# A decoder step on one core: the conditioning of tiles 5 to 7 in one visit of eight weight blocks, of tiles 8 to 15 in two of eight

## The chip, the cores and the metric

The kernel runs on one core of one Trainium2 chip. The metric is the device time of one execution in microseconds (us), from the first to the last thing that the core does; it is given as the median of several runs.

## The reference, cut to what matters

One layer of a decoder runs over 288 tokens: 256 of a prompt and 8 groups of 4 samples. Each group of tokens (9 in all) has a conditioning vector `c`, from which one matrix product makes six vectors of 2048 numbers per group; they scale, shift and gate the features (2048 = 16 tiles of 128).

```python
mod = (jax.nn.silu(c) @ w_ada + b_ada).reshape(n, N_MOD, 1, D_MODEL)   # w_ada: 2048 x 12288
sh_m, sc_m, gt_m, sh_f, sc_f, gt_f = [mod[:, i] for i in range(N_MOD)]
h = _rms(x, g_mix) * (1 + sc_m) + sh_m
proj = h @ w_in                                                        # 2048 x 9216
```

Behind it come a short convolution, a spatial gate, three products that merge them (`w_pa`, `w_pb`, `w_out`) and a feed-forward block (`w_ffn_in`, `w_ffn_out`). All is float32. The change concerns the first two lines and the product with `w_in`.

## The kernel before, in words

**Main blocks.** A weight matrix is cut into parts of 128x128. A block (class `Blk`) is 12 to 16 such parts, fetched by one DMA of SP into one of 7 raw buffers (tag "raw", `RAW = 7`, 1024 KB each). `Blk.split` then makes of each 4 parts a high half (ACT, line 480) and a low half (DVE; line 258 while these engines run in the order in which the program is written, else 487), into 4 "hi" and 4 "lo" buffers of 4 parts each (`SPB = 4`). The raw buffer is free when the last low half is made. PE takes one part with three matmuls (`triple`, lines 239, 242 and 244): high by high, high by low, low by high, 288 columns each.

**Conditioning blocks.** Class `Ada` does the product with `w_ada`. The unit aD makes the scales and shifts of tiles 5 to 7, in 8 blocks of 768 KB (two of the 16 input tiles each); aE makes those of tiles 8 to 15, in 16 blocks of 1024 KB (one input tile each). PE reads these straight from the raw buffer (line 412): a block is 8 matmuls of 192 columns each in aD and 4 of 512 in aE, counted twice that in the profile's rows, which list weight loads and matmuls; the buffer is free when PE has read it. A run of such blocks between main blocks is called a visit. When a unit's last block is done, `tail` (later, on DVE) adds the bias, and `mk_h1` makes the modulated input tiles `h1`, which the following main blocks read.

**Order.** The product with `w_in` goes over input tiles in the order in which they become ready: `w0`, `wK`, `wA` (tiles 0 to 1, then 2 to 3), `wB` (six blocks of 12 parts, tiles 2 to 4), `wX` (six of 12, tiles 5 to 7), `wS` (five of 14, tiles 1 to 7), `wC` (19 of 12, tiles 2 to 7), then `wE`, `wF`, `wD`. The function `at` puts visits behind the n-th main block of a list. Before the change they are: 4 blocks of aD behind wB1, 4 behind wB3; 5 blocks of aE behind wX3, 6 behind wS4, 5 behind wC6. All of it lies in the first 215 us.

**Loads.** `stream` is the order in which PE uses blocks, `order` that in which SP fetches them. When step i of the stream is written, load i + 7 of `order` is issued, so that each load waits for one of the 7 buffers. In the loop at line 1201 some main blocks are put in front of the visit that they follow, so that they can be fetched and split ahead of it: wA3, wA4, wA5 and wC0.

**Splits.** Up to the step `free` (behind the last visit of aE) the splits are placed by hand: `feed` writes the next split into ACT's and DVE's order when the parts that are split and unused have come down to the block's `lead`, 12 unless set (wC1 has 7); the low half is written two parts later (`LAG`). Evictions of PE's results and the jobs of `pre_h1` and `mk_h1` (line 318 scales one tile) stand in the same two queues.

Of the kernel before, what the change touches and what calls it, by code (L numbers as in the profile page):

```python
# [88 lines left out]
def decoder_kernel(tc, d):  # L89
    nc = tc.nc  # L90
    from contextlib import ExitStack

    with ExitStack() as es:
        def pool(name, bufs=1, **kw):
            return es.enter_context(tc.tile_pool(name=name, bufs=bufs, **kw))

        pc = pool("const")
        pw = pool("wstream")
        pslot = pool("slots", MAIN)
        pkept = pool("kept", KEPT)  # L100
        ptmp = pool("tmp", 5)
        pps = pool("psum", 4, space=bass.MemoryType.PSUM)
        with tc.manual_schedule(engines={nc.tensor.engine}):
            _body(tc, nc, d, pc, pw, pslot, pkept, ptmp, pps)


def _body(tc, nc, d, pc, pw, pslot, pkept, ptmp, pps):
# [208 lines left out]
    def normed(kt, rb):  # L316
        t = slot()
        V.tensor_tensor(t, x[:, kt, :], rb, ALU.mult)
        return t

    def modulate(ks, get, gm, sh0, out):
        hs, his = {}, {}

        def affine(k, t):
            h = tmp()
            hi = slot(F32R)
            A.activation(
                h[:, :TP], t[:, :TP], AF.Identity, bias=mod[:, sh0 + k, 0:1], scale=gm[:, k, 0:1]
            )
            V.tensor_tensor(sam(h[:, TP:]), sam(t[:, TP:]), bc4(gm[:, k, 1:]), ALU.mult)  # L330
            V.tensor_tensor(sam(h[:, TP:]), sam(h[:, TP:]), bc4(mod[:, sh0 + k, 1:]), ALU.add)
            A.copy(hi, h)
            hs[k], his[k] = h, hi

        def finish_(k):
            lo = slot(F32R)
            V.tensor_tensor(lo, hs[k], his[k].bitcast(F32), ALU.subtract)
            out[k] = (his[k], lo)

        ts = {}  # L340
        n = len(ks)
        for i in range(n + 2):
            if i < n:
                ts[i] = get(ks[i])
            if 1 <= i <= n:
                affine(ks[i - 1], ts.pop(i - 1))
            if i >= 2:
                finish_(ks[i - 2])
# [241 lines left out]
    def ada(name):  # L590
        u = units[name]
        return [Ada(u, b) for b in range(16 // u[2])]
# [8 lines left out]
    def warm(n, out=None):  # L601
        out = idle if out is None else out
        for _ in range(n):
            PE.matmul(out[:, :T], wb[:, :P], wb, start=True, stop=True)
# [46 lines left out]
    def pre_h1(k0, k1):  # L651
        def scaled(k):
            def f():
                made[k] = normed(k, S["rb1"])

            return f

        return Do(lambda: jobs.extend(scaled(k) for k in range(k0, k1)), None)

    def make_h1(k0, k1):  # L660

        def scaled(k):
            made[k] = normed(k, S["rb1"])

        def affine(k):
            t, h = made[k], tmp()
            A.activation(h[:, :TP], t[:, :TP], AF.Identity, bias=mod[:, k, 0:1], scale=gm1[:, k, 0:1])
            V.tensor_tensor(sam(h[:, TP:]), sam(t[:, TP:]), bc4(gm1[:, k, 1:]), ALU.mult)
            V.tensor_tensor(sam(h[:, TP:]), sam(h[:, TP:]), bc4(mod[:, k, 1:]), ALU.add)
            made[k] = h  # L670

        def high(k):
            hi = slot(F32R)
            A.copy(hi, made[k])
            made[k] = (made[k], hi)

        def low(k):
            h, hi = made.pop(k)
            lo = slot(F32R)
            V.tensor_tensor(lo, h, hi.bitcast(F32), ALU.subtract)  # L680
            h1[k] = (hi, lo)

        def job(i):
            def f():
                for at, part in enumerate(parts):
                    if k0 <= i - at < k1:
                        part(i - at)

            return f

        parts = (affine, high, low) if k0 in made or jobs else (scaled, affine, high, low)
        jobs.extend(job(i) for i in range(k0, k1 + len(parts) - 1))
# [47 lines left out]
    def gm_of(k0, k1):  # L740
        V.scalar_tensor_tensor(
            gm1[:, k0:k1, :],
            mod[:, 16 + k0 : 16 + k1, :],
            1.0,
            gmix[:, k0:k1].unsqueeze(2).to_broadcast([P, k1 - k0, NC]),
            ALU.add,
            ALU.mult,
        )

    def mk_h1(k0, k1):  # L750
        def f():
            gm_of(k0, k1)
            if S.get("paced") is not None:
                return make_h1(k0, k1)
            modulate(range(k0, k1), lambda k: normed(k, S["rb1"]), gm1, 0, h1)

        return Do(f)
# [3 lines left out]
    def sinkA(m, ps):  # L761
        wide = m < ROOTLESS and m not in LONG
        t = kept() if m in LONG else slot(shape=(P, TU) if wide else (P, T))
        part[m] = t[:, :T]
        w = TU if wide else T
        copy = A.copy if (m not in ON_VECTOR if m < ROOTLESS else m % 2 or m % 8 == 4) else V.tensor_copy
        copy(t[:, :w], ps[:, :w])
        if m < ROOTLESS:
            i = 0 if wide else LONG.index(m)
            e = t[:, T:] if wide else (extra + [extra2])[i // 4][:, i % 4]  # L770
            raws[m] = t, e
            if not wide:
                copy(e, ps[:, T:TU])

    def sinkC(m, ps):
        if m not in raws:
            return sinkB(m, ps)
        t, e = raws.pop(m)
        V.scalar_tensor_tensor(t[:, :TP], ps[:, :TP], e[:, :1], t[:, :TP], ALU.add, ALU.add)  # L779
        rescale(m + 4, V.tensor_tensor(t[:, TP:T], ps[:, TP:T], t[:, TP:T], ALU.add))  # L780
# [7 lines left out]
    def sinkX(m, ps):  # L788
        after = sinkB(m, ps)
        if m >= 68:  # L790
            rescale(m - 68, after)

    def sinkB(m, ps):
        return V.tensor_tensor(part[m], ps[:, :T], part[m], ALU.add)  # L794
# [307 lines left out]
    def at(main, plan):  # L1102
        out, n = [], 0
        for s in main:
            out.append(s)
            if isinstance(s, Blk):
                n += 1
                out += plan.pop(n, [])
        assert not plan
        return out  # L1110

    a0, a1, aC, aD, aE = ada("a0"), ada("a1"), ada("aC"), ada("aD"), ada("aE")
# [6 lines left out]
    wA = [Blk("wA", i, (xe if i < many else h1).__getitem__, lambda m, ps: sinkA(FIRST + m, ps)) for i in range((72 - FIRST) // 8)]  # L1119
    wB = [Blk("wB", i, rh1, lambda m, ps: sinkB(LATER + m, ps)) for i in range((72 - LATER) // 4)]  # L1120
    wX = [Blk("wX", i, rh1, lambda m, ps: sinkX(LATER + m, ps)) for i in range((72 - LATER) // 4)]
    wS = [Blk("wS", i, rh1, sinkC) for i in range(SINGLE // 2)]
    wC = [Blk("wC", i, rh1, lambda m, ps: sinkC(SINGLE + m, ps)) for i in range((LATER - SINGLE) // 2)]
    for b in wA[:many]:
        b.width = TU
    wC[1].lead = 7
    w0.cut = 512
    wK.cut = 384
    w0.lead, wK.lead, wA[0].lead, wA[1].lead = 6, 3, 6, 8
# [2 lines left out]
    steps = [Do(lambda: warm(19)), a0[0], Do(lambda: warm(5)), a0[1]]  # L1132
# [5 lines left out]

    plan = {4: [Do(root, None)], 5: aC[:2], 6: aC[2:5] + [pre_h1(2, 5)], 7: aC[5:] + [mk_h1(2, 5)]}
    steps += at([w0, wK] + wA, plan)  # L1140
    steps += at(wB, {2: aD[:4], 3: [pre_h1(5, 8)], 4: aD[4:] + [mk_h1(5, 8)]})
    free = Do(lambda: None, None)
    steps += at(wX + wS + wC, {4: aE[:5], 11: aE[5:11], 18: aE[11:] + [free, mk_h1(8, 12), mk_h1(12, 16)]})

    def wD(m0, m1):
        return [Blk("wD", i, rh1, sinkD) for i in range(m0 // 2, m1 // 2)]
# [51 lines left out]
    stream = [s for s in steps if not isinstance(s, Do) and not s.apart]  # L1198
    pos = {id(s): i for i, s in enumerate(stream)}
    order = list(stream)  # L1200
    for unit, blk in ((aC[:2], wA[3]), (aC[2:5], wA[4]), (aC[5:], wA[5]), (aE[5:11], wC[0])):
        order.remove(blk)
        order.insert(order.index(unit[0]), blk)
    head = contextlib.ExitStack()
# [163 lines left out]
```

## Time and profile before

| | |
|---|---|
| median of 3 runs | 1591.73 us (1591.66 to 1592.06) |
| the profiled execution | 1592.19 us, of which its span 1590.4 us |
| PE busy | 1579.8 us, 99% of the span |
| PE weight loads, DVE, ACT busy | 96%, 64%, 46% |
| DMA | 357.89 MB, 225 GB/s over the span |

The span is the time from the first to the last instruction of the profiled execution; the rest of its 1592.19 us lies around it. PE's matmuls are pipelined, and a busy PE may still issue late: a delay shows as a longer step from one matmul's start to the next. The chain is the list of work that set the end, followed back from the last instruction. Times in the rows are microseconds from the span's start.

### The profile page before, as it was taken

How to read it: one execution, taken by the hardware profiler on the slowest of the kernel's cores; microseconds unless marked ns; L12 is line 12 of the kernel's file. 1: busy time of each engine (PE TensorE's matmuls, PEld its weight loads, DVE VectorE, ACT ScalarE, POOL GpSimd, SP SyncE). 2: the span in 40 equal slices, each digit the busy share in tenths (PEclk: the TensorE clock that was granted, in tenths of full speed). 3: DMA queues.
4: the chain of work that ended last, by engine and by line, in shares of the span. 5: the costliest groups of instructions: out<-in, count | busy, mean ns of one | idle time of the engine just before them, and what ended most of it. 6: DMA issues, size and time to landing. Idle time of an engine off the chain costs nothing.

```text
span 1590.4 us, 31810 instructions
## 1 busy us (share of the span) xinstructions
PE 1579.8 (99%) x12700; PEld 1519.9 (96%) x12700; DVE 1014.4 (64%) x2200; ACT 736.2 (46%) x1366; POOL 21.4 (1%) x65
## 2 busy tenths in 40 slices
PE   9999999999999999999999999999999999999997
PEld 8999899998999989899898999999999999999997
DVE  6777788877755758567844555555555555555565
ACT  6633344643444435356643444444444444444464
POOL 0000000000000000011000000000000000000000
PEclk9999999999999999999999999999999999999999
DMA  9887876777767778784757356453564534645341
GB/s 382 333 331 281 306 261 217 276 290 296 291 231 266 309 290 264 273 295 164 295 182 275 128 181 212 161 176 113 171 230 159 176 120 164 231 159 175 113 165 60
DMA packets 67685, 357.89 MB, mean 225 GB/s; under 512 B 7632, under 2 KB 19536, under 8 KB 37840
## 3 DMA queue, kind: packets, MB, share of 16 engines
q1 hardware_dynamic: 67248, 355.73, 61.6%
q8 instruction: 99, 1.62, 0.4%
q14 instruction: 50, 0.41, 0.1%
q10 hardware_dynamic: 288, 0.13, 0.0%
HBM read 352.74 MB, written 3.09 MB: 224 GB/s over the span
## 4 chain that ended last, share of the span: by engine, by line
PE 98%; DMA 1%; DVE 0%; DVEq 0%; ACT 0%; issue 0%; ACTq 0%
PE pm L239 31%; PE pm L244 31%; PE pm L242 30%; PE ada L412 5%; DMA raw<-in_wK 1%; DMA raw<-in_w 0%; DVE st L1079 0%; DMA t<-in_c 0%; PE px L242 0%; PE px L239 0%; PE px L244 0%; PE px L911 0%; PE px L910 0%; PE px L857 0%; PE px L213 0%; PE px L1051 0%
## 5 line engine op out<-in xcount | busy, mean ns | idle before, releaser
L239 PE MATMUL pm<-s,hi 128*128 128x288 f32 (+1 forms) x3750 | 1094.8, 292 | 0.0
L242 PE MATMUL pm<-s,hi 128*128 128x288 f32 (+1 forms) x3750 | 1090.5, 291 | 0.0
L244 PE MATMUL pm<-s,lo 128*128 128x288 f32 (+1 forms) x3738 | 1088.1, 291 | 0.0
L480 ACT CAST hi<-raw 128x512 fp32r<-128x512 f32 (+1 forms) x963 | 585.5, 610 | 777.9 <-PE pm L242 743.5
L487 DVE TENSOR_TENSOR lo<-raw,hi 128x512 fp32r<-128x512 f32 (+1 forms) x849 | 577.5, 682 | 408.6 <-ACT hi L480 396.1
L239 PEld LDWEIGHTS pm<-s,hi 128*128 128x128 f32 x3750 | 702.1, 187 | 11.7 <-issue 9.9
L242 PEld LDWEIGHTS pm<-s,hi 128*128 128x128 f32 x3750 | 702.2, 187 | 0.0
L244 PEld LDWEIGHTS pm<-s,lo 128*128 128x128 f32 x3738 | 699.9, 187 | 0.0
L258 DVE TENSOR_TENSOR lo<-raw,hi 128x512 fp32r<-128x512 f32 x111 | 74.4, 676 | 19.8 <-ACT hi L480 18.7
L412 PE MATMUL ada<-raw,cs 128*32 128x512 f32 (+2 forms) x1088 | 80.7, 444 | 1.0 <-DMA raw<-in_a 0.6
L412 PEld LDWEIGHTS ada<-raw,cs 128*32 128x32 f32 x1088 | 29.1, 110 | 41.9 <-issue 37.5
L802 DVE TENSOR_TENSOR s<-pm,s 128x288 f32<-128x288 f32 x72 | 32.8, 456 | 16.3 <-PE pm L244 16.1
L311 ACT CAST s<-t 128x288 fp32r<-128x288 f32 (+1 forms) x76 | 32.9, 433 | 15.6 <-DVE t L834 9.4
L313 DVE TENSOR_TENSOR s<-t,s 128x288 fp32r<-128x288 f32 (+1 forms) x76 | 35.0, 460 | 6.0 <-ACT s L311 5.2
L353 DVE SCALAR_TENSOR_TENSOR x<-pm,mod,x 128x256 f32<-128x256 f32 x79 | 37.6, 475 | 0.0
L1000 DVE SCALAR_TENSOR_TENSOR t<-t,pm 128x288 f32<-128x288 f32 x42 | 19.1, 455 | 19.6 <-PE pm L244 19.6
L794 DVE TENSOR_TENSOR s<-pm,s 128x288 f32<-128x288 f32 x48 | 21.8, 454 | 10.8 <-PE pm L244 10.0
L352 DVE TENSOR_TENSOR t<-pm,mod 128x32 f32<-128x32 f32 x79 | 15.1, 192 | 20.1 <-PE pm L244 19.5
L779 DVE SCALAR_TENSOR_TENSOR s<-pm,s 128x256 f32<-128x256 f32 x36 | 17.3, 481 | 8.3 <-PE pm L244 8.3
L785 DVE TENSOR_TENSOR s<-s,rb 128x288 f32<-128x288 f32 x48 | 21.6, 449 | 0.0
L181 ACT ACTIVATE t<-x 128x288 f32<-128x288 f32 x29 | 12.9, 444 | 17.6 <-DVE x L356 17.6
L186 DVE TENSOR_TENSOR acc<-acc,t 128x288 f32<-128x288 f32 x33 | 15.0, 455 | 8.2 <-ACT t L181 8.2
(170 smaller groups left out, 489.0 us busy)
## 6 DMA issues: line engine op xcount, KB each, us to landing
raw<-in_fi SPq DMA_DIRECT2D x84, 1024.0 KB, 4.8
raw<-in_a SPq DMA_DIRECT2D x56, 1024.0 KB, 5.0
raw<-in_f SPq DMA_DIRECT2D x64, 704.0 KB, 4.0
raw<-in_wD SPq DMA_DIRECT2D x34, 1024.0 KB, 6.7
raw<-in_aE SPq DMA_DIRECT2D x16, 1024.0 KB, 7.0
raw<-in_wo SPq DMA_DIRECT2D x16, 1024.0 KB, 6.0
raw<-in_wC SPq DMA_DIRECT2D x19, 768.0 KB, 6.5
raw<-in_pa SPq DMA_DIRECT2D x8, 1024.0 KB, 9.7
```

The lines of the kernel that those rows point to most:

```text
L239: PE.matmul(out, wh, ah, start=first, stop=False)
L242: end_ = PE.matmul(out, wh, al, start=False, stop=turn and last)
L244: end_ = PE.matmul(out, wl, ah, start=False, stop=last)
L258: lows.pop(0)[1]()
L311: A.copy(hi, a)
L313: V.tensor_tensor(lo, a, hi.bitcast(F32), ALU.subtract)
L353: V.scalar_tensor_tensor(x[:, m, :TP], ps[:, :TP], mod[:, gt0 + m, 0:1], x[:, m, :TP], ALU.mult, ALU.add)
L412: PE.matmul(acc[32 * j : 32 * j + 32, h * w // n : (h + 1) * w // n], cs[:, kt, :], self.held[2 * j + h] if self.held else self.raw[:, o : ...
L480: A.copy(hi, self.raw[:, s * 128 : e * 128])
L487: sub()
L794: return V.tensor_tensor(part[m], ps[:, :T], part[m], ALU.add)
L802: V.tensor_tensor(a, ps[:, :T], a, ALU.add)
```

## The change

The two visits of aD become one of eight blocks behind wB3; the three of aE become two of eight, behind wS4 and wC6. wB4 is now fetched ahead of the visit of aD and wC7 ahead of the second of aE; wC0 stays ahead of the first. wB5 and wC8, like wC1 before, are split when 7 unused parts are left instead of 12. The steps that make h1 stand where they stood.

```diff
@@ -1123,7 +1123,7 @@
-    wC[1].lead = 7
+    wB[5].lead = wC[1].lead = wC[8].lead = 7
@@ -1138,9 +1138,9 @@
-    steps += at(wB, {2: aD[:4], 3: [pre_h1(5, 8)], 4: aD[4:] + [mk_h1(5, 8)]})
+    steps += at(wB, {3: [pre_h1(5, 8)], 4: aD + [mk_h1(5, 8)]})
     free = Do(lambda: None, None)
-    steps += at(wX + wS + wC, {4: aE[:5], 11: aE[5:11], 18: aE[11:] + [free, mk_h1(8, 12), mk_h1(12, 16)]})
+    steps += at(wX + wS + wC, {11: aE[:8], 18: aE[8:] + [free, mk_h1(8, 12), mk_h1(12, 16)]})
@@ -1198,7 +1198,7 @@
-    for unit, blk in ((aC[:2], wA[3]), (aC[2:5], wA[4]), (aC[5:], wA[5]), (aE[5:11], wC[0])):
+    for unit, blk in ((aC[:2], wA[3]), (aC[2:5], wA[4]), (aC[5:], wA[5]), (aD, wB[4]), (aE[:8], wC[0]), (aE[8:], wC[7])):
```

## Rows read from the trace of the kernel before

**Rows 1.** The page, part 1: span, and busy time of each engine.
```profile
span 1590.4 us, 31810 instructions
...
PE 1579.8 (99%) x12700; PEld 1519.9 (96%) x12700; DVE 1014.4 (64%) x2200; ACT 736.2 (46%) x1366; POOL 21.4 (1%) x65
```
**Rows 2.** The page, part 4: the chain that ended last, by engine.
```profile
PE 98%; DMA 1%; DVE 0%; DVEq 0%; ACT 0%; issue 0%; ACTq 0%
```
**Rows 3.** The chain in order of time: start, us, what; visits and a matmul behind one.
```profile
43.37 1.44 PE ada L412 x32
...
84.46 2.74 PE ada L412 x64
87.20 0.33 PE pm L239
...
127.67 4.43 PE ada L412 x40
...
168.85 5.29 PE ada L412 x48
```
**Rows 4.** Stretches: us, PE, PEld, DVE, ACT, POOL busy (instructions), clock, DMA share, GB/s.
```profile
100.00:125.00 25.00, 25.00 (x195) 25.00 (x194) 22.49 (x54) 12.20 (x22) 0.00 (x0) 1.00 0.85 329
```
**Rows 5.** All waits of PE's matmuls for a load, in the whole span: us, times, longest.
```profile
PE ada L412 <- DMA raw<-in_a: 0.6, 1, 0.6
```
**Rows 6.** Timeline of PE: start and length of three visits.
```profile
84.39 2.81 PE L412 MATMUL ada<-raw,cs 128*32 128x192 f32 x64
...
168.78 5.36 PE L412 MATMUL ada<-raw,cs 128*32 128x512 f32 x48
...
206.93 4.50 PE L412 MATMUL ada<-raw,cs 128*32 128x512 f32 x40
```
**Rows 7.** Waits of SP's queue around visits (84.9 to 85.6; 166 to 169.6).
```profile
SPq L385 <- PE ada L412: 0.5, 1, 0.5
...
SPq L463 <- DVE lo L258: 3.6, 1, 3.6
```
**Rows 8.** Timeline of DVE near visits: low halves, and a scaling job.
```profile
83.70 0.68 DVE L258 TENSOR_TENSOR lo<-raw,hi 128x512 fp32r<-128x512 f32 x1
...
97.23 0.45 DVE L318 TENSOR_TENSOR s<-x,rb 128x288 f32<-128x288 f32 x1
...
168.63 0.69 DVE L258 TENSOR_TENSOR lo<-raw,hi 128x512 fp32r<-128x512 f32 x1 [0.69 <-ACT hi L480]
...
206.14 0.68 DVE L258 TENSOR_TENSOR lo<-raw,hi 128x512 fp32r<-128x512 f32 x1
```
**Rows 9.** Timeline of SP: the loads issued as these buffers came free.
```profile
169.35 0.33 SPq L463 DMA_DIRECT2D raw<-in_wC  x1
...
206.85 0.33 SPq L463 DMA_DIRECT2D raw<-in_wC  x1
```
**Rows 10.** DMA issues, us to landing; issued at 169.35, 169.91, 165.33, 836.86, 837.72, 287.34, 287.99.
```profile
raw<-in_wC SPq DMA_DIRECT2D x1, 768.0 KB, 4.1
...
raw<-in_wC SPq DMA_DIRECT2D x1, 768.0 KB, 5.5
...
raw<-in_aE SPq DMA_DIRECT2D x1, 1024.0 KB, 4.7
...
raw<-in_fi SPq DMA_DIRECT2D x1, 1024.0 KB, 4.9
...
raw<-in_fi SPq DMA_DIRECT2D x1, 1024.0 KB, 6.7
...
raw<-in_wD SPq DMA_DIRECT2D x1, 1024.0 KB, 4.8
...
raw<-in_wD SPq DMA_DIRECT2D x1, 1024.0 KB, 7.3
```
**Rows 11.** Stretches at the end, behind PE's last matmul; columns as in rows 4.
```profile
1583.00:1585.00 2.00, 0.00 (x0) 0.00 (x0) 2.00 (x3) 0.00 (x0) 0.00 (x0) 1.00 0.85 330
1585.00:1587.00 2.00, 0.00 (x0) 0.00 (x0) 1.71 (x2) 0.00 (x0) 0.00 (x0) 0.55 1.01 406
```

## The prediction

> **What bounds the kernel now.** I read the page's busy times first: PE is busy for 1579.8 of the span's 1590.4 us [rows 1]. A busy PE can still issue late, so the chain of waits comes next: 98% of the span lies on PE [rows 2]. In a stretch between visits PE starts 195 matmuls in 25.00 us, one per 0.128 us, while DVE is busy for 22.49 us and ACT for 12.20 [rows 4]. The list of waits has one wait of PE for a load, 0.6 us, in the head of the kernel, and none from 40 us on [rows 5]. So every load and every split is hidden, and a microsecond in which PE waits is a microsecond of the end.
>
> What a visit costs beyond its work is read from the chain in order of time [rows 3]. Six blocks of aE take 5.29 us and five 4.43, so one takes 0.86, and 5.29 - 6 x 0.86 leaves 0.13 for entering. Four blocks of 768 KB take 2.74 us and two (aC, of the same size) 1.44, so one takes 0.65, and 0.14 is left. The first matmul behind a visit takes 0.33 instead of 0.13, 0.20 more. A visit thus costs 0.33 us, and this is all that two fewer can give.
>
> Last I read SP's queue. Behind a visit's start its loads end their waits on "PE ada" or on "DVE lo" [rows 7]: a conditioning block's buffer comes free when PE has read it, a main block's when its last low half is made. There are 7 buffers, and no visit before reads more than 6 blocks from them.
>
> **The change part by part.**
>
> *Two visits fewer.* 2 x 0.33 = 0.66 us less. The matmuls, bytes and loads stay the same in number, as do the bias steps and the makers of h1; only their places differ.
>
> *Eight blocks through seven buffers.* This is the part that decides. At a visit's start the main block behind it has been fetched first and holds one buffer until it is split; six hold blocks 1 to 6. Block 7 can only go into the buffer of that main block, and block 8 into the one that PE gives back after block 1. SP issues in order, so block 8 stands behind block 7 in any case, and the main blocks behind the visit stand behind both. Times below are from the visit's first matmul [rows 6]; without a wait PE comes to block 7 and 8 of aD at 6 x 0.65 = 3.9 and 4.55, of aE at 5.16 and 6.0.
>
> When the main block's buffer comes free: a high half needs one of four buffers that PE must have left, so the last third of a 12-part block cannot be made before PE is four parts from the end of the block ahead, however early the data is there. Three visits show it. Ahead of the one at 84.39 the last low half ends at 83.70 + 0.68, just at its start. At 168.78 the low half ends 0.54 behind the start and SP issues at +0.57; at 206.93 it ends 0.11 ahead and SP issues at -0.08 [rows 6, 8, 9]. The second aE visit still follows a 14-part wS block and the third a 12-part wC block, so +0.57 and -0.08 are taken over. For aD the first value holds, with one scaling job of h1 more in front of it on DVE (0.45, some 0.37 of it not overlapped) [rows 8]: issue at +0.4. Nothing frees it sooner; a busier DVE could only free it later.
>
> How long a load takes: alone, 768 KB landed after 4.1 us and 1024 KB after 4.7 to 4.9. A second one issued right behind landed 1.95 later (169.91 + 5.5 against 169.35 + 4.1) for 768 KB, and 2.66 (837.72 + 6.7 against 836.86 + 4.9) or 3.15 (287.99 + 7.3 against 287.34 + 4.8) for 1024 KB [rows 10]. I take 4.2 and 1.95, 4.8 and 2.6; another 0.07 passes until PE starts (an estimate; it is too small to matter).
>
> - aD: block 7 lands at 0.4 + 4.2 = 4.6, 0.7 late; block 8 at 6.55, and PE starts it at 6.6 instead of 4.55: **2.1 us** of waiting in all.
> - First aE visit: block 7 at 0.57 + 4.8 = 5.4, 0.2 late; block 8 at 8.0, started at 8.05 instead of 6.0: **2.05 us**.
> - Second aE visit: block 7 at -0.08 + 4.8 = 4.7, in time; block 8 at 7.3, started at 7.4: **1.4 us**.
>
> Together 5.55 us of new waits, less 0.66: **+4.9 us**. Bounds by the rows: the short ends are 4.1 and 4.7, and a second landing 0.15 to 0.2 sooner than in these pairs (they were issued 0.56 and 0.86 apart, here it is 0.35 to 0.55); the waits are then 1.8 + 1.8 + 1.15 = 4.75, net +4.1. With 4.3 and 2.6, 4.9 and 3.2 they are 2.8 + 2.75 + 2.1 = 7.65, net +7.0.
>
> [...]
>
> *wB4, wC7 fetched earlier.* wB4 goes ahead of eight blocks of aD, of which SP issues all but the last two before the visit; PE uses block 6 of aD at 3.25, and its buffer (wB3's) is free one whole block earlier, some 4.7 us before the visit, so it has landed. The same holds for block 6 of aE. No cost. The cover is one main block of 12 parts x 3 x 0.128 = 4.6 us.
>
> *wB5, wC1, wC8 behind block 8, split at 7.* While SP waits for block 7's buffer, all later loads stand behind it. wB5 lands some 1.9 us behind block 8, so about 1.2 us into wB4, which lasts 4.6; its first four parts are split within some 1.4 us (0.69 of it on DVE [rows 8]), and PE wants it 2 us later still. wC1 and wC8 likewise, with 2.5 for 1.9. Hidden, at nothing; if DVE, 90% busy there [rows 4], is late with it, up to 1 us more per place, which goes into the upper end.
>
> *Fewer loads bunched elsewhere.* wX4 to wC0 no longer wait behind five blocks of aE. PE waited for none of them, so nothing is gained.
>
> The profiled execution took 1592.19 us, its span 1590.4 with 1.8 around it; +4.9 makes 1597.1. The median of the runs is 0.46 below that execution, so against it the sum is 1591.73 + 4.9 = **1596.6 us**, 0.31% more. (A difference under 0.2%, 3.2 us, can't be told from none here.)
>
> **The rivals.**
>
> - *Block 7 is in time, so the visits of eight pass without a wait: not slower.* The place is the buffer of wB4, wC0 and wC7, the price -0.66 us: 1591.1 us. It decides where that buffer comes free some 2.1 us before the visit, or where the pool gives block 7 and 8 other buffers that are free by then. For it: a block's own landing from its own buffer (PE reads block 1 by 1.1, + 4.8 = 5.9) would just make 6.0, so only the queueing behind block 7 is in the way. Against it: the four high buffers, and the low halves at 168.63 and 206.14 [rows 8]. 11%.
> - *Loads shorter than the rows.* If each block 7 lands 0.4 us sooner and each block 8 another 0.2, three visits wait 3 x 0.6 = 1.8 less: 5.55 - 1.8 - 0.66 = +3.1, 1594.8 us, on the edge of what can be told. Against it: none of the first loads in [rows 10] is so short, and six would have to be. 7%. [...]
> [...]
> - *Something outside (the scheduler's order behind the last visit, where ACT and DVE are no longer ordered by hand) gains or loses more.* PE has no other wait to lose [rows 5], so a gain of 0.2% finds no place. 1%.
>
> **How the numbers follow.** The three waits have 78%; their bounds are +4.1 to +7.0, and with up to 1 us for late splits 1595.8 to 1599.7. The likeliest single value is 1596.6. The range goes down past the shorter loads, to 1594.3, and up to 1600.0: it leaves out the rival without waits (11%), the clock (3%) and the odd tails. Slower by over 0.2%: the 78, the 3 and half of the 7, less a tail, 83%. Within 0.2%: the 11, the rest of the 7, 16%. Faster: 1%.
>
> **What the changed profile would show.** The list of waits should have PE at line 412 waiting for raw<-in_aD (two waits, 2 us together) and raw<-in_aE (two to four, 3.4 us). SP's load of block 7 should end its wait on "DVE lo" within 0.6 us of each visit's start, and block 8 be issued right behind it and land 2 to 3 us later. The chain's pieces for the visits should be about 7.3, 9.0 and 8.4 us, where eight blocks alone take 5.3 and 7.0. The clock should stay at 1.00, and matmuls behind the visits at 0.128 us. I am wrong if block 7 is issued more than 2 us before a visit, if PE waits at fewer than three visits, or if the waits add up to under 3.8 us.

## The result and the profile after

The changed kernel takes 1599.4 us in the median of six runs (1597.4 to 1603.55), the kernel before 1591.89 (six runs, 1591.66 to 1592.47) on the same chip: a ratio of 1.005, interval 1.0037 to 1.0063. It is slower by 7.5 us, where 4.9 were forecast. The runs spread over 6 us, where the kernel before spreads over 0.8.

The profiled execution is the quickest of the six, 1597.40 us, 5.2 more than the profiled one before. Its page has the same busy time of PE in a span 5.2 us longer, against [rows 1]:

```profile
span 1595.6 us, 31807 instructions
...
PE 1579.7 (99%) x12700; PEld 1519.3 (95%) x12700; DVE 1013.8 (64%) x2200; ACT 735.7 (46%) x1366; POOL 21.4 (1%) x65
```

The list of PE's waits between 40 and 420 us was empty before [rows 5]. Now it has conditioning blocks, and nothing else (us in total, times, longest):

```profile
PE ada L412 <- DMA raw<-in_aE: 3.3, 2, 1.9
PE ada L412 <- DMA raw<-in_aD: 1.9, 2, 1.3
```

The chain in order of time (start, us, what), beside [rows 3]. It leaves PE in each visit: it goes back from the eighth block to that block's load and, past the load, to the first block, whose buffer the load took.

```profile
93.42 1.15 PE ada L412 x25
94.58 5.59 DMA raw<-in_aD
100.21 0.86 PE ada L412 x16
101.07 0.33 PE pm L239
...
165.82 1.06 PE ada L412 x9
166.88 6.65 DMA raw<-in_aE
173.57 1.07 PE ada L412 x8
174.64 0.33 PE pm L239
...
207.50 1.04 PE ada L412 x8
208.56 6.98 DMA raw<-in_aE
215.58 1.06 PE ada L412 x8
216.65 0.33 PE pm L239
```

From its start to the first main matmul a visit lasts 101.07 - 93.42 = 7.65, 8.82 and 9.15 us. Without waits eight blocks take 5.34 (8 x 0.65 + 0.14) and 7.0 us. So the waits are 2.3, 1.8 and 2.15 us, 6.25 in all. (The list of waits has 5.2: it counts the idle time from the modelled end of a matmul on, and shows no wait of its own for block 7 of aE.) Less the 0.66 of two visits that is 5.6, and a head that ran 0.35 sooner here (aC's third visit begins at 59.90 instead of 60.25 in the chain) leaves the 5.2.

The timeline of SP gives the issues of blocks 7 and 8 in the three visits:

```profile
93.75 0.33 SPq L385 DMA_DIRECT2D raw<-in_aD  x1
...
94.58 0.33 SPq L385 DMA_DIRECT2D raw<-in_aD  x1
...
166.32 0.33 SPq L385 DMA_DIRECT2D raw<-in_aE  x1
...
166.88 0.91 SPq L385 DMA_DIRECT2D raw<-in_aE  x1
...
207.35 0.33 SPq L385 DMA_DIRECT2D raw<-in_aE  x1
...
208.56 0.33 SPq L385 DMA_DIRECT2D raw<-in_aE  x1
```

And the DMA view their landings, in us from issue, for the two of aD and for block 8 of each aE visit (block 7 of aE landed after 4.8 twice):

```profile
raw<-in_aD SPq DMA_DIRECT2D x1, 768.0 KB, 4.3
...
raw<-in_aD SPq DMA_DIRECT2D x1, 768.0 KB, 5.6
...
raw<-in_aE SPq DMA_DIRECT2D x1, 1024.0 KB, 6.7
...
raw<-in_aE SPq DMA_DIRECT2D x1, 1024.0 KB, 7.0
```

Block 7 is issued 0.4, 0.57 and -0.08 us from the visits' first matmuls (93.36, 165.75, 207.43 in the timeline of PE), the values read from [rows 8, 9]. Block 8 follows 0.6 to 1.2 later and lands 2.1 to 3.4 behind block 7. SP's own waits in the visit of aD tell what each of the two was held by:

```profile
SPq L385 <- DVE lo L258: 4.6, 1, 4.6
...
SPq L385 <- PE ada L412: 0.8, 1, 0.8
```

Block 7 waits for the last low half of the main block, and block 8 for PE's reading of block 1. The visits of aE have the same two waits. So block 8 goes out at 1.22, 1.13 and 1.13 us from the visit's start, however early block 7 went.

### The profile page after: what moved, and what is told of

Same layout as the page of the kernel before. It is cut to its first block, busy times and chain, and to the rows that moved or that the text cites. A ratio compares the mean times of both kernels' runs of the same rounds, so it can differ in the third digit from the quotient of the medians.

```text
span 1595.6 us, 31807 instructions
## 1 busy us (share of the span) xinstructions
PE 1579.7 (99%) x12700; PEld 1519.3 (95%) x12700; DVE 1013.8 (64%) x2200; ACT 735.7 (46%) x1366; POOL 21.4 (1%) x65
## 4 chain that ended last, share of the span: by engine, by line
PE 97%; DMA 2%; DVE 0%; DVEq 0%; issue 0%; ACT 0%; ACTq 0%
PE pm L239 31%; PE pm L244 30%; PE pm L242 30%; PE ada L412 4%; DMA raw<-in_aE 1%; DMA raw<-in_wK 1%; DMA raw<-in_aD 0%; DMA raw<-in_w 0%; DVE st L1079 0%; DMA t<-in_c 0%; PE px L242 0%; PE px L239 0%; PE px L244 0%; PE px L911 0%; PE px L910 0%; PE px L857 0%
## 5 line engine op out<-in xcount | busy, mean ns | idle before, releaser
L426 DVE STREAM_TRANSPOSE ev<-ada 128x512 f32<-128x512 f32 (+2 forms) x9 | 4.8, 536 | 28.1 <-PE ada L412 28.1
```

## The experiments

They were run in three groups, each on one chip together with the kernel before (median 1591.8 to 1591.9 in each group). Two questions: are blocks 7 and 8 the cause, and where do the other 2 us of the median and the spread come from.

**The change again**, unaltered.

> The changed kernel once more, unaltered, to see why its six runs spread over 6 us (1597.4 to 1603.55) where the kernel before spread over 0.8. Theory C (clock): some of the new waits bring PE's clock down for a while in some executions; then the runs' times go with their mean granted clock, some 1.6 us for each 0.001 of it, and a profile of a long run shows a stretch below 1.00 behind a visit of eight. Rival L (loads): in long runs blocks 7 and 8 land later; then the mean clock of a long run is that of a short one, and the waits in the visits are longer. Both expect a median near 1599 and the three waits of the first profile (2.3, 1.8 and 2.15 us).

It measured 1600.74 us (1598.37 to 1602.31). The profiled execution, 1601.21, is long on both accounts. Its visits last 8.4, 9.9 and 9.5 us, so the waits are 3.0, 2.9 and 2.5, 8.4 in all, 2.1 more than in the first profile: the landings differ between executions. The chain has the loads of block 8, from issue to landing, at

```profile
94.63 6.34 DMA raw<-in_aD
...
167.68 7.73 DMA raw<-in_aE
...
210.44 7.34 DMA raw<-in_aE
```

where the first profile has 5.59, 6.65 and 6.98. And behind the third visit the clock falls. In its stretches (us, PE, PEld, DVE, ACT, POOL busy, clock, DMA share, GB/s) PE has 4 matmuls in the 2 us up to 218, then 21 in 4 us, then 32:

```profile
216.00:218.00 2.00, 0.18 (x4) 0.16 (x8) 0.00 (x0) 0.00 (x0) 0.00 (x0) 1.00 1.01 394
218.00:222.00 4.00, 4.00 (x21) 3.19 (x14) 2.39 (x10) 1.22 (x3) 0.00 (x0) 0.61 1.01 420
222.00:226.00 4.00, 4.00 (x32) 4.00 (x31) 2.79 (x8) 3.17 (x7) 0.00 (x0) 0.96 1.02 424
```

4 us at 0.61 and 4 at 0.96 lose 1.7 us. 8.4 + 1.7 - 0.66 = 9.4, and the run is 9.3 over the median before. Both theories hold a part. Over the eleven runs of the change the time goes with the mean granted clock: 1597.4 and 1598.4 us at 0.999, 1598.6 and 1598.7 at 0.998, 1600.0 to 1601.2 in the five at 0.997, 1602.3 and 1603.6 at 0.996. The long runs are the ones with falls of the clock, then, but the falls are not all of it: of the 3.8 us between the two profiled executions the landings make 2.1 and the one fall 1.7.

**One half of the change at a time.** Only aD in one visit:

```diff
-    steps += at(wX + wS + wC, {11: aE[:8], 18: aE[8:] + [free, mk_h1(8, 12), mk_h1(12, 16)]})
+    steps += at(wX + wS + wC, {4: aE[:5], 11: aE[5:11], 18: aE[11:] + [free, mk_h1(8, 12), mk_h1(12, 16)]})
```

(with the fetches and leads of before for wC; lines against the changed kernel)

> Only the aD part of the change: one visit of eight for tiles 5 to 7, aE in three visits as before. Seven-buffer theory: one visit of 0.33 us less, a wait of 2.1 us (2.3 in the first profile of the change), so +1.8 to +2.0 us against the kernel before, 1593.8, if the clock holds; spread up to 2 us more under theory C if this wait is one that lowers the clock. Rival (the cost is in the order of loads or in the later splits, not in blocks 7 and 8): no wait at aD's blocks, waits elsewhere.

It measured 1594.22 us (1593.84 to 1596.19), +2.3; ratio 1.0016, interval 1.0008 to 1.0025. PE's only waits are the two of aD:

```profile
PE ada L412 <- DMA raw<-in_aD: 2.0, 2, 1.4
```

The profiled execution, 1595.48, has a fall of the clock from this visit's last block on (0.50 in the 3 us from 100.5, in which the chain steps by 0.24 per matmul); runs with a mean clock of 0.999 took 1593.84 and 1594.11, +1.9 and +2.2, where 1.8 to 2.0 was expected.

Only aE in two visits of eight:

```diff
-    steps += at(wB, {3: [pre_h1(5, 8)], 4: aD + [mk_h1(5, 8)]})
+    steps += at(wB, {2: aD[:4], 3: [pre_h1(5, 8)], 4: aD[4:] + [mk_h1(5, 8)]})
```

(with the fetch and lead of before for wB; lines against the changed kernel)

> Only the aE part: two visits of eight for tiles 8 to 15, aD in two visits as before. Seven-buffer theory: 0.33 us less, waits of 1.8 to 2.05 and 1.4 to 2.15 us, so +3.1 to +3.6 us against the kernel before, about 1595.4, if the clock holds. Theory C: a spread of some us above that, going with the mean clock, if these waits are the ones that lower it. Rival L: the same spread with the clock at 1.00 throughout.

It measured 1599.74 us (1595.61 to 1602.8), +7.8; the quickest, with a mean clock of 0.998, is at +3.7, the 3.1 to 3.6 expected and a tenth more. The profiled one has waits of 3.1 and 2.3 us, and two falls:

```profile
173.50:176.50 3.00, 3.00 (x15) 2.80 (x12) 0.00 (x0) 0.62 (x1) 0.00 (x0) 0.50 1.02 426
177.00:181.00 4.00, 4.00 (x33) 4.00 (x33) 3.17 (x9) 1.60 (x3) 0.00 (x0) 1.00 1.02 427
...
218.00:221.00 3.00, 3.00 (x15) 3.00 (x14) 2.23 (x11) 2.06 (x4) 0.00 (x0) 0.50 1.02 425
```

The waits of aE carry most of the loss and of the spread. (The two halves add up to 10.1 us where the whole took 8.8 on this chip; with five runs that spread over 7 us, the shares are rough.)

**No eighth block.** Five visits again, of at most seven, with the early fetches (their list, not shown, follows the visits) and the late splits of the change:

```diff
-    steps += at(wB, {3: [pre_h1(5, 8)], 4: aD + [mk_h1(5, 8)]})
+    steps += at(wB, {2: aD[:1], 3: [pre_h1(5, 8)], 4: aD[1:] + [mk_h1(5, 8)]})
-    steps += at(wX + wS + wC, {11: aE[:8], 18: aE[8:] + [free, mk_h1(8, 12), mk_h1(12, 16)]})
+    steps += at(wX + wS + wC, {4: aE[:2], 11: aE[2:9], 18: aE[9:] + [free, mk_h1(8, 12), mk_h1(12, 16)]})
```

> Five visits as before, but of 1 and 7 blocks of aD and of 2, 7 and 7 of aE, with wB4, wC0 and wC7 fetched ahead and the later splits as in the change: no visit has an eighth block. Seven-buffer theory: only block 7 can be late, by 0.75 us in aD, 0.3 in the first visit of seven of aE and 0 in the second: +1.05 us, 1592.9, and a spread as small as before's. Rival (order of loads, later splits, longer visits as such): most of the change's loss stays, +4 us or more.

It measured 1593.05 us (1592.94 to 1593.45), +1.1 where 1.05 was expected (ratio 1.0008, interval 0.9999 to 1.0017), and the spread is gone. What is left of the waits is block 7's:

```profile
PE ada L412 <- DMA raw<-in_aD: 0.5, 1, 0.5
PE ada L412 <- DMA raw<-in_aE: 0.2, 1, 0.2
```

Longer visits, early fetches and late splits cost nothing that shows; the eighth block costs the rest.

**An eighth buffer**, for the change and for the kernel before. Room for it comes from column tiles 64 to 71 of the product with `w_in`, which share one tile in these two kernels, so that their results are overwritten; the work is the same. The cut shows one of the four places where `RAW` becomes `RAW + 1`; its last line lets two later units fetch one block fewer into the kept tiles, of which there are now seven fewer:

```diff
-KEPT = 36
+KEPT = 29
...
-            self.raw = pw.tile([P, n], F32, tag="raw", name=nm("raw"), bufs=RAW, padded_shape=[P, 2048])
+            self.raw = pw.tile([P, n], F32, tag="raw", name=nm("raw"), bufs=RAW + 1, padded_shape=[P, 2048])
...
+        if m == 64:
+            S["one"] = kept()
-        t = kept() if m in LONG else slot(shape=(P, TU) if wide else (P, T))
+        t = S["one"] if m >= 64 else kept() if m in LONG else slot(shape=(P, TU) if wide else (P, T))
...
-        for i, b in enumerate(unit[12:]):
+        for i, b in enumerate(unit[13:]):
```

> The change with eight raw buffers instead of seven; to make room, the results of the last eight column tiles of w_in (64 to 71) share one tile, so these are not computed rightly, at the same work. Seven-buffer theory: block 7 takes a buffer that is free a whole main block earlier, block 8 the one of the main block fetched ahead, so it lands 4.6, 5.4 and 4.7 us behind the visits' starts where PE wants it at 4.55, 6.0 and 6.0: waits of 0.1 us in all, the loss of the change gone, 0.5 us less than the same kernel with the visits of before (e8_before8). Rival (long visits, the order of loads or the later splits cost by themselves): +4 us or more against e8_before8. Clock: no wait, so no stretch below 1.00 ahead of the end, and a spread under 1 us.

> The control for e4_eight: the kernel before, with eight raw buffers and the same sharing of one tile by column tiles 64 to 71 (not computed rightly, same work). No wait of PE existed with seven, so an eighth gives nothing: within 0.5 us of the kernel before, unless the shared tile makes the evictions of tiles 64 to 71 wait, which would be seen in e4_eight as well.

The change measured 1591.72 us (1591.44 to 1592.51), the control 1592.19 (1591.91 to 1593.12): 0.47 less, where 0.5 was expected, though the intervals of their ratios to the kernel before (0.999 to 1.0008; 0.9993 to 1.0011) overlap. PE has no wait between 40 and 420 us, and the chain stays on PE through every visit:

```profile
93.91 5.52 PE ada L412 x128
99.43 0.33 PE pm L239
164.19 7.00 PE ada L412 x64
171.19 0.33 PE pm L239
204.05 7.00 PE ada L412 x64
211.06 0.33 PE pm L239
```

Here the visits of eight last 5.52 and 7.00 us, and the mean clock is 0.998 or 0.999 in all eleven runs, as in the kernel before. That the buffers are the cause is shown from both sides: one block fewer, or one buffer more. Without that shared tile no room for an eighth buffer was found, so no version that beats the kernel before came out of this.

**Work in the waits.**

```diff
+            if self.fill:
+                warm(self.fill, psmain())
...
+    aD[7].fill, aE[7].fill, aE[15].fill = 8, 10, 12
```

> The change with 8, 10 and 12 matmuls without use put ahead of the eighth block of aD and of the two visits of aE, so that PE works for 1.0 to 1.5 us of each wait. The block cannot start before it has landed in any case. Clock theory: the waits stay (6 to 8 us in all), but no stretch behind a visit falls below 1.00 any more: the median goes down by 1 to 3 us, to about 1597.5 to 1598.5, the mean clock is 0.998 to 0.999 in every run, and what spread is left goes with the landings. Rival (the spread is of the landings alone): the median stays near 1600.

It measured 1598.39 us (1597.9 to 1599.37), +6.5, with a spread of 1.5. The change itself took +8.8 in the repeated run and +7.5 in the first six. The mean clock is 0.998 or 0.999 in all five runs, as in every run of the kernel before; in seven of the change's eleven it is 0.997 or less. (The intervals of the ratios overlap, 1.0029 to 1.0054 against 1.0041 to 1.0066 and 1.0037 to 1.0063, so it is the clock that shows the effect, and not the median alone.) The timeline of PE in the first aE visit shows the ten matmuls in the wait, and block 8 behind them:

```profile
171.75 1.06 PE L415 MATMUL ada<-raw,cs 128*32 128x512 f32 x8 [0.30 <-DMA raw<-in_aE]
172.75 1.40 PE L607 MATMUL pm<-wb 128*128 128x288 bf16 x10
174.21 1.06 PE L415 MATMUL ada<-raw,cs 128*32 128x512 f32 x8
175.20 0.39 PE L239 MATMUL pm<-s,hi 128*128 128x288 f32 x1
```

The visits last 8.1, 9.1 and 9.2 us, so the eighth blocks come 7.0 us late in all, between the 6.25 and 8.4 of the change: 1591.86 + 7.0 - 0.66 = 1598.2, and the profiled run took 1598.10. The waits' length is the landings'. With work in them the clock is 1.00 through the three visits and in the 3.7 to 4.0 us behind each, where the repeated run of the change has 0.61 behind the third: in these profiles it fell, behind a visit, only where PE had nothing to do in the wait.

**No main block ahead of aE's visits**, so that seven blocks fit.

```diff
-    wB[5].lead = wC[1].lead = wC[8].lead = 7
+    wB[5].lead = 7
+    wC[0].lead = wC[7].lead = -1
...
-    steps += at(wX + wS + wC, {11: aE[:8], 18: aE[8:] + [free, mk_h1(8, 12), mk_h1(12, 16)]})
+    steps += at(wX + wS + wC, {11: aE[:8] + [back(0)], 18: aE[8:] + [back(7), free, mk_h1(8, 12), mk_h1(12, 16)]})
...
-    for unit, blk in ((aC[:2], wA[3]), (aC[2:5], wA[4]), (aC[5:], wA[5]), (aD, wB[4]), (aE[:8], wC[0]), (aE[8:], wC[7])):
+    for unit, blk in ((aC[:2], wA[3]), (aC[2:5], wA[4]), (aC[5:], wA[5]), (aD, wB[4])):
```

(`back`, not shown, sets the lead to 12 and splits what has been fetched)

> The aE part with no main block fetched ahead: wC0 and wC7 come behind the eight blocks and are split when they land. Seven-buffer theory: seven blocks are in at a visit's start, the eighth goes into the first one's buffer (issued at +1.1) and lands alone, at +5.9, where PE wants it at 6.0, so the waits inside aE's visits go; but wC0 and wC7 land about 7.9 behind the start and are split 1.4 later, where PE wants them at 7.1: some 2.2 us of waiting behind each visit instead. In all about the change's time, 1591.9 + 2.1 + 4.4 - 0.7 = 1597.7 without the clock's part. Rival (the loss is in the visits themselves): the waits inside them stay.

It measured 1599.15 us (1597.81 to 1599.91); the quickest two, with a clock of 0.999, are a tenth above the 1597.7 expected. The waits inside aE's visits are gone, and PE waits behind them for the halves of wC0 and wC7:

```profile
PE pm L239 <- ACT hi L480: 2.9, 2, 1.5
PE ada L412 <- DMA raw<-in_aD: 2.5, 2, 1.4
PE pm L244 <- DVE lo L258: 0.4, 2, 0.2
```

That is 3.3 us of idle time where 4.4 us of delay was expected. In the profiled run aD's visit lasted 8.35 us, 3.0 more than eight blocks alone, where 2.1 was expected, and the clock fell once. The eighth blocks of aE, with no block 7 just ahead of them, landed in time: the list has no wait for raw<-in_aE. Who holds the seventh buffer only decides where PE waits.

**All of aE in one visit.**

```diff
-    steps += at(wX + wS + wC, {11: aE[:8], 18: aE[8:] + [free, mk_h1(8, 12), mk_h1(12, 16)]})
+    steps += at(wX + wS + wC, {11: aE, 18: [free, mk_h1(8, 12), mk_h1(12, 16)]})
```

(with aD, its fetch and the leads of before, and wC0 fetched ahead of the visit; line against the changed kernel)

> All sixteen blocks of aE in one visit behind wS4 (wC0 fetched ahead), aD in two visits as before: two visits fewer than before, the suspected cost doubled and more. Seven-buffer theory: blocks 1 to 6 are in, block 7 lands 5.4 us behind the visit's start and block 8 at 8.0, and from there on a block every 2.45 us at the loads' own pace, the sixteenth at 27.6, where PE alone would want it at 12.9: 14.7 us of waits, +14.0 us against the kernel before, 1605.9, if the clock holds; one fall of the clock behind the visit adds 1.7, and if PE's work of 0.86 in each 2.45 us is too little to keep the clock within the visit, some us more. Rival (a fixed cost of a visit of eight, of order or split): about +4 us, as for two visits of eight.

It measured 1607.99 us (1607.23 to 1609.96), +16.2 (ratio 1.0099, interval 1.0083 to 1.0116) against +14.0 for the waits and 1.7 per fall. From the eighth block on PE starts one every 2.45 us, as each load lands. Its stretches show the clock low within the visit, up for a while, and low again:

```profile
176.00:180.00 4.00, 3.48 (x16) 0.20 (x8) 0.00 (x0) 0.00 (x0) 0.00 (x0) 0.50 1.01 426
...
184.00:188.00 4.00, 2.08 (x18) 0.17 (x10) 0.00 (x0) 0.00 (x0) 0.00 (x0) 0.90 1.01 426
...
192.00:196.00 4.00, 3.48 (x17) 1.41 (x14) 1.03 (x4) 0.00 (x0) 0.00 (x0) 0.50 1.01 422
```

While each block waits for its load a low clock costs little: a block takes 1.9 us instead of 1.06 (its four matmuls from start to end) and still fits into 2.45. It costs at the last block and behind the visit.

## Why the prediction was right, and where it was short

- *What bounds the kernel.* Right: PE had no slack, and the 6.25 us of waits in the first profile stand in its time in full, less 0.66.
- *Two visits fewer, -0.66.* Borne out by the pair with eight buffers, -0.47 beside some 0.18 of waiting in aD (5.52 - 5.34), though the difference lies within the intervals.
- *When the buffer of the main block comes free.* Right in all three visits: +0.4, +0.57, -0.08.
- *When block 8 is issued.* **This step was short.** The prediction put block 8 into the buffer that PE gives back after block 1, and had block 1 read by 1.1 (in its first rival), but then let it follow block 7 by 0.35 to 0.55 us. It followed by 0.83, 0.56 and 1.21. The third visit, the second of aE, shows it best: from the visit's start block 7 went out 0.65 sooner there than in the second visit, block 8 no sooner, and the wait was 2.15 instead of the 1.4 forecast, no shorter than the second visit's 1.8.
- *How long a load takes.* The first landings were right (4.3, 4.8, 4.8 against 4.2, 4.8, 4.8). **The term that was mis-sized is the second landing**, taken 1.95 and 2.6 us behind the first. It came 2.1, 2.45 and 3.4 later in the first profile. There the 3.4 exceeds the 2.45 of the visit before mostly by the later issue: from their own issues the two loads took 7.0 and 6.7 us. In the repeated run the loads of block 8 themselves took longer (6.34, 7.73 and 7.34). In all the waits are 6.25 to 8.4 us where 5.55 were taken; the upper bound of 7.65 was too low as well. The rows had the late pair (3.15), but as an end, not as the common case. That a first load lands 0.4 us sooner than taken and a second another 0.2, to which the range reaches down, no run shows. Nor does one show the 0.07 from landing to PE's start, an estimate: in the first profile PE started 0.04 us behind each landing of block 8 (94.58 + 5.59, then 100.21).
- *The clock, at 3%.* **The other step that failed**: the forecast had it stay at 1.00, and the one gap of PE that the rows show with its clock lies at the kernel's end [rows 11]. In these visits it did fall, in some executions, from 1.00 to 0.50: in the profiled runs twice for the aE half and in the visit of sixteen, once for the aD half, the repeated change and the kernel without a main block ahead, never in the kernels without an eighth block late or with work in the wait. Behind a visit of eight it rose again soon: the fall in the repeated run lost 1.7 us, one with 0.50 for 3 us loses about 1.5 (an estimate from the stretches of the two halves). With work in the waits the loss is 6.5 us instead of 7.5 to 8.8, so the falls' share of the median is perhaps 1 to 2.3 us (an estimate).
- *wB5, wC1 and wC8 late.* Nothing: no PE wait behind a visit in the changed kernel.
- *Not slower.* Fell with the waits. Its argument, that the eighth block would be in time if it did not queue behind the seventh, was right, as the kernel without a main block ahead shows; but then the main block is late.
- *The number.* That the first median, 1599.4, lies within the 1594.3 to 1600.0 of the forecast is in part luck: the same kernel's second group of runs has its median at 1600.74, above it. The mechanism was right, and its own share, 5.6 us in the first profile and 7.8 in the repeated one, was forecast at 4.9.

What stays open is why the clock falls in one execution and not in another: it held through the waits of 2.3, 1.8 and 2.15 us in the first profile and through those of 3.0 and 2.9 in the repeated run, and fell there behind 2.5. It is as open why a second load takes 6.7 us from its issue in one execution and 7.7 in another.

## What to carry to other kernels

Count who holds each buffer at the moment a long run of blocks begins: the buffers, less the one of the block fetched ahead, are the blocks that may run without a wait. Here the next one, block 7, was late by up to half a microsecond (the kernel without an eighth block), and the one after it, block 8, had to land behind a queue; the two cost about six times what a visit saved. Ask too when each of their loads can be issued, not only in which order. A merge that saves a third of a microsecond per switch pays only while the run still fits. And price a short wait of TensorE with what it may do to the clock behind it (here 1.5 to 1.7 us where it fell), or give it work there.

## What the runs showed that was not expected

Waits of two to three microseconds spread the times of a kernel that otherwise repeats to 0.05%: by loads of block 8 that take 0.4 to 1.1 us longer in one execution than in another (6.34, 7.73 and 7.34 us against 5.59, 6.65 and 6.98), and by falls of the granted clock from 1.00 to 0.50 behind a visit, about 1.5 to 1.7 us each. In the visit of sixteen, where PE waited in each 2.45 us, the clock was low for about 17 of the visit's 30 us; in the kernel before, whose visits of the same blocks have no wait, it was 1.00 from 168.78 to 174.10 us and from 206.93 to 211.40.
